# Loading modulation weights as bf16, moving border matmuls, and reading the post-norm factor from PSUM in a two-layer conv/attention step on eight cores

## The chip, the cores and the metric

The kernel runs on the eight cores of one Trainium2 chip. Each core works on its own batch element, with no exchange between cores. The metric is device time in microseconds (us) of the slowest core, as the median of several executions. Some executions fall into a slow state, in which the cores of one die or both show a lower granted TensorE clock. Those executions are set aside, and only fast runs are compared.

A word on names. TensorE is PE, its weight loads are PEld, VectorE is DVE, ScalarE is ACT, and GpSimd is POOL. SyncE is SP, which here only issues DMAs. "Pool queue" means the DMAs that POOL issues. Only these convert f32 to bf16 on the way in this kernel.

## The reference

Each core has three units of 1024 tokens: S0 and S1 (two halves of one latent sequence) and P (four context sequences of 256). There are two layers. Layer 0 mixes tokens with a gated convolution, layer 1 with attention. Each is followed by a gated ConvFFN.

```python
mod = silu(c) @ mod_w[i] + mod_b[i]            # 6 parts of 1024: shift, scale, gate, twice
u = rms_norm(h, g_pre) * (1 + scale) + shift
y = short_conv_mixer(u) or block_attention(u) @ w_o
h = h + gate * rms_norm(y, g_post)             # the "tail" below
u = rms_norm(h, g_pre2) * (1 + scale2) + shift2
g, up = split(dwconv3(u @ w_up))               # 2 x 2816 columns
h = h + gate2 * rms_norm((silu(g) * up) @ w_down, g_post2)
```

The width-3 convolution couples S0 and S1 at one column, the border. Whichever unit is computed first needs one column of its neighbour. For each weight block, "border matmuls" with a single right-hand column compute it.

## The kernel before

All operations go into a list scheduler written in Python. It estimates durations and fixes each engine's order. Engines execute in that order and wait on semaphores. Stages follow each other: conv input and conv output for S0, S1, P; FFN input and output for S1, P, S0; the attention stretch; then FFN input and output for S0, S1, P again. Five parts matter here.

Modulation weights in the prologue come as f32 over SP and are cast by ACT and DVE:

```python
def mod_stage(l, blks):
    ...
        P.dma("sp", d[blk][0], modw[l, blk], 128 * 8192, writes=d[blk][1])
# in mod_gen:
    if blk % 2: P.act(2048, "sb", sk, wk, w, src, AF.Copy)
    else:       P.dve(lambda e, ...: e.tensor_copy(out=w, in_=src), 1024, sk, wk)
```

FFN input takes its weights from a ring of 23 KB per partition, 4 KB per block. Border matmuls get a scheduling priority 18 us later than their block and hold its weight slot until they have run:

```python
for c in range(NCF):                       # 22
    w, wk = load_w(wup[l, c], KC * 256)    # pool queue, f32 -> bf16
    for s in range(2):
        zmm(b, ub, ..., wk, halo=s * 22 + c, late=18.0)   # 16 matmuls of 128x512
        P.act(1024, "ps", ..., r, z, AF.Copy, scale=...)
        taps(U, r, z, ...)                                # two DVE ops that read PSUM
```

The tail of every output phase scales y with rs, the reciprocal RMS. It reads rs from SBUF, and POOL adds the result to h:

```python
rs = rs_t[:, (2 + ct) * 512:(3 + ct) * 512]
rstd_ops(6 + ct, 512, D, rs, rk)           # ACT: Ln, then Exp
for m in range(KC):
    P.dve(... e.scalar_tensor_tensor(out=y, in0=y, scalar=cf[...], in1=rs, op0=mult, op1=mult) ...)
    P.pool(... tensor_tensor(out=hh, in0=hh, in1=y, op=add) ...)
```

The last output phase runs column half by column half and loads every weight twice. The modulation blocks of layer 0 are spread like this:

```python
stage(conv_in(S0, UU, True), ..., (mod_gen(0, [2, 3]), 1, 0.8), (load_h(S1, x_in, 1), 0, 0.5))
stage(conv_in(S1, UU, False), ..., (mod_gen(0, [4]), 2, 1.0), (load_h(PU, x_in, 0), 3, 0.5))
stage(conv_in(PU, UU, False), ..., (mod_gen(0, [5]), 0, 1.0))
```

## Time and profile before

The median was 2769.04 us. The profiled execution took 2773.4 us on core 5, the slowest. These lines of the page show the busy time of each engine, the granted TensorE clock in 40 slices (9 means 90 to 99 per cent), and four groups of instructions. A group gives line, engine, operation, output and inputs, shape and count, then total busy us, mean ns of one, and the idle time before them.

```profile
PE 2549.2 (92%) x13935; PEld 1167.3 (42%) x13935; DVE 1466.2 (53%) x1497; ACT 1303.9 (47%) x1739; POOL 1021.2 (37%) x971
...
PEclk9999999989999999999999999999999999999998
...
L606 PE MATMUL ps<-u,wr 128*128 128x512 bf16 x5376 | 1208.3, 385 | 85.3 <-DVE ra L631 23.4
...
L549 DVE SCALAR_TENSOR_TENSOR yb<-yb,coef,rs 128x512 f32<-128x512 f32 x96 | 127.7, 1360 | 248.3 <-ACT rs L100 248.3
...
L549 DVE SCALAR_TENSOR_TENSOR ev<-ev,coef,rs 128x512 f32<-128x512 f32 x80 | 110.3, 1409 | 178.6 <-ACT rs L100 178.6
...
L553 POOL TENSOR_TENSOR h<-h,yb 128x512 f32<-128x512 f32 x92 | 135.4, 1483 | 68.4 <-DVE yb L549 67.9
```

The clock line: a 9 stands for 90% or more of full speed.

The view of PE's waits for the same core gives who was waited for, total us, times and the longest wait:

```profile
PE ps L606 <- DVE ra L631: 23.4, 20, 3.7
PE ps L606 <- DMA wr<-win: 18.8, 6, 4.9
PE ps L606 <- DMA wr<-wup: 17.9, 5, 4.7
PE ps L384 <- ACT u L100: 15.1, 4, 5.3
```

L606 is the projection matmul of the conv and FFN inputs. It waits for tap results on DVE, for conv weights (win) and for FFN weights (wup). L384 is the modulation matmul, which waits for ACT's casts.

### The profile page before, as it was taken

How to read it: one execution, taken by the hardware profiler on the slowest of the kernel's cores; microseconds unless marked ns; L12 is line 12 of the kernel's file. 1: busy time of each engine (PE TensorE's matmuls, PEld its weight loads, DVE VectorE, ACT ScalarE, POOL GpSimd, SP SyncE). 2: the span in 40 equal slices, each digit the busy share in tenths (PEclk: the TensorE clock that was granted, in tenths of full speed). 3: DMA queues.
4: the chain of work that ended last, by engine and by line, in shares of the span. 5: the costliest groups of instructions: out<-in, count | busy, mean ns of one | idle time of the engine just before them, and what ended most of it. 6: DMA issues, size and time to landing. Idle time of an engine off the chain costs nothing.

```text
span 2773.4 us, 38402 instructions; the slowest of 8 cores (2744.9 to 2773.4 us)
## 1 busy us (share of the span) xinstructions
PE 2549.2 (92%) x13935; PEld 1167.3 (42%) x13935; DVE 1466.2 (53%) x1497; ACT 1303.9 (47%) x1739; POOL 1021.2 (37%) x971
## 2 busy tenths in 40 slices
PE   1899999889999999998997999999999999999997
PEld 0344444444444444443443444434444444444443
DVE  2446565856189638726524223243285618736743
ACT  2133324434255434436665777777543434434432
POOL 1124241734074335415425233240163316425423
PEclk9999999989999999999999999999999999999998
DMA  8557654344467545634235000100334355536456
GB/s 232 121 92 154 128 91 80 65 84 75 75 145 152 101 70 98 106 53 83 50 58 179 12 12 9 28 1 1 61 54 84 65 104 122 126 63 136 85 91 145
DMA packets 75368, 242.13 MB, mean 87 GB/s; under 512 B 9264, under 2 KB 12848, under 8 KB 74160
## 3 DMA queue, kind: packets, MB, share of 16 engines
q0 software_dynamic: 48368, 171.99, 36.8%
q1 hardware_dynamic: 26816, 67.69, 7.3%
q8 instruction: 115, 1.88, 0.3%
q14 instruction: 69, 0.57, 0.1%
HBM read 382.25 MB, written 29.36 MB: 148 GB/s over the span
## 4 chain that ended last, share of the span: by engine, by line
PE 74%; DVE 8%; DMA 7%; issue 7%; ACT 3%; POOL 1%; SPq 1%; DVEq 0%; ACTq 0%; POOLq 0%
PE ps L606 30%; PE ps L576 22%; PE ps L915 5%; PE ps L923 5%; DVE ra L631 3%; PE ps L795 3%; DMA wr<-win 2%; PE ps L932 2%; PE ps L957 2%; PE ps L585 1%; PE ps L826 1%; PE ps L484 1%; DMA yb<-modw 1%; DMA wr<-wup 1%; DVE yb L549 1%
## 5 line engine op out<-in xcount | busy, mean ns | idle before, releaser
L606 PE MATMUL ps<-u,wr 128*128 128x512 bf16 x5376 | 1208.3, 385 | 85.3 <-DVE ra L631 23.4
L606 PEld LDWEIGHTS ps<-u,wr 128*128 128x128 bf16 x5376 | 525.7, 99 | 734.8 <-issue 140.1
L576 PE MATMUL ps<-ra,wr 128*128 128x512 bf16 x2624 | 596.7, 381 | 9.2 <-DMA wr<-wdn 6.8
L631 DVE SCALAR_TENSOR_TENSOR ev<-ps,par,ev 128x1023 f32<-128x1023 f32 (+1 forms) x336 | 427.8, 1280 | 194.6 <-ACT ev L100 162.4
L576 PEld LDWEIGHTS ps<-ra,wr 128*128 128x128 bf16 x2624 | 257.3, 98 | 324.1 <-issue 20.2
L100 ACT ACTIVATE wr<-ps 128x1024 bf16<-128x1024 f32 (+1 forms) x352 | 333.6, 984 | 98.8 <-PE ps L915 96.1
L100 ACT ACTIVATE ev<-ps,par 128x1024 f32<-128x1024 f32 x168 | 186.8, 1112 | 278.8 <-PE ps L606 276.4
L549 DVE SCALAR_TENSOR_TENSOR yb<-yb,coef,rs 128x512 f32<-128x512 f32 x96 | 127.7, 1360 | 248.3 <-ACT rs L100 248.3
L712 POOL TENSOR_TENSOR ra<-ev 128x1023 bf16<-128x1023 f32 (+1 forms) x84 | 199.8, 2379 | 146.9 <-DVE ev L631 66.5
L631 DVE SCALAR_TENSOR_TENSOR ra<-ps,par,ra 128x1023 f32<-128x1023 f32 (+1 forms) x192 | 239.0, 1272 | 21.4 <-ACT ra L100 12.2
L549 DVE SCALAR_TENSOR_TENSOR ev<-ev,coef,rs 128x512 f32<-128x512 f32 x80 | 110.3, 1409 | 178.6 <-ACT rs L100 178.6
L491 DVE SCALAR_TENSOR_TENSOR tm<-h,coef,rs 128x512 f32<-128x512 f32 x192 | 146.5, 799 | 72.6 <-ACT rs L100 72.4
L923 PE MATMUL ps<-wr,ra 128*128 128x512 bf16 x640 | 175.6, 383 | 2.1 <-DVE ra L944 2.1
L482 POOL TENSOR_TENSOR sqa<-h 128x512 bf16<-128x512 f32 x104 | 117.4, 1140 | 136.5 <-PE ps L484 80.0
L100 ACT ACTIVATE sqb<-ps 128x512 bf16<-128x512 f32 x236 | 139.9, 597 | 58.8 <-PE ps L795 43.7
L553 POOL TENSOR_TENSOR h<-h,yb 128x512 f32<-128x512 f32 x92 | 135.4, 1483 | 68.4 <-DVE yb L549 67.9
L100 ACT ACTIVATE ra<-ps,par 128x1024 f32<-128x1024 f32 x96 | 106.4, 1110 | 102.9 <-PE ps L606 69.4
L100 ACT ACTIVATE yb<-ps 128x512 f32<-128x512 f32 x112 | 66.8, 596 | 183.8 <-PE ps L576 183.2
L113 POOL DMA_DIRECT2D wr<-wup x132 | 74.9, 569 | 201.3 <-PE ps L585 145.0
L553 POOL TENSOR_TENSOR h<-h,ev 128x512 f32<-128x512 f32 x80 | 114.3, 1443 | 37.9 <-DVE ev L549 37.4
L712 POOL TENSOR_TENSOR ra<-ra 128x1023 bf16<-128x1023 f32 (+1 forms) x48 | 115.8, 2412 | 30.3 <-ACT ra L100 18.7
L100 ACT ACTIVATE ev<-ps 128x512 f32<-128x512 f32 x80 | 47.6, 596 | 167.4 <-PE ps L576 163.7
(134 smaller groups left out, 2364.4 us busy)
## 6 DMA issues: line engine op xcount, KB each, us to landing
wr<-wup POOLq DMA_DIRECT2D x132, 512.0 KB, 6.0
wr<-wdn POOLq DMA_DIRECT2D x56, 704.0 KB, 7.6
wr<-modw POOLq DMA_DIRECT2D x40, 512.0 KB, 7.0
wr<-win POOLq DMA_DIRECT2D x24, 768.0 KB, 9.1
h_mem<-h SPq DMA_DIRECT2D x24, 512.0 KB, 5.5
h<-h_mem SPq DMA_DIRECT2D x24, 512.0 KB, 5.7
h_out<-h SPq DMA_DIRECT2D x48, 256.0 KB, 4.2
h<-x_in SPq DMA_DIRECT2D x16, 512.0 KB, 10.2
```

The lines of the kernel that those rows point to most:

```text
L100: return self._add("act", lambda e: e.activation(out=out, in_=in_, func=func, **kw), reads, writes, busy, busy + 0.12, table=self.TABLES.g ...
L482: P.pool(lambda e, s=s, src=src: e.tensor_tensor(out=s, in0=src, in1=src, op=ALU.mult), 512, hk(U, kc, ct), [("sqa", i)])
L491: P.dve(lambda e, kc=kc, t=t, rs=rs, src=hap(U, kc, ct * 512, ct * 512 + 512): e.scalar_tensor_tensor(out=t, in0=src, scalar=cf[:, ai, kc, ...
L549: P.dve(lambda e, y=y, m=m, rs=rs: e.scalar_tensor_tensor(out=y, in0=y, scalar=cf[:, gi, m, U.v:U.v + 1], in1=rs, op0=ALU.mult, op1=ALU.mu ...
L553: fa = lambda e, y=y, hh=hh: e.tensor_tensor(out=hh, in0=hh, in1=y, op=ALU.add)
L576: ins = e.matmul(bank(b), w3[:, k, :], rhs_fn(k, ct), start=(k == 0), stop=(k == nk - 1))
L606: ins = e.matmul(bank(b + ct), lhs_fn(kc), ub.ap[:, kc, ct * 512:ct * 512 + 512], start=(kc == 0), stop=(kc == KC - 1))
L631: P.dve(lambda e, ro=ro, zi=zi, w=w: e.scalar_tensor_tensor(out=ro, in0=zi, scalar=w, in1=ro, op0=ALU.mult, op1=ALU.add), 1024, rd + wr, wr)
L712: P.pool(lambda e, rg=rg, ru=ru, c=c: e.tensor_tensor(out=a3(c, c0, c1), in0=rg[:, c0:c1], in1=ru[:, c0:c1], op=ALU.mult), 1024, rgk + ruk ...
L795: ins = e.matmul(bank(b), w3[:, kc, :], ub.ap[:, kc, ct * 512:ct * 512 + 512], start=(kc == 0), stop=(kc == KC - 1))
L915: ins = e.matmul(o, K[:, j, k0:k0 + 128], rhs, start=True, stop=True)
L923: ins = e.matmul(bank(ob + a), V[:, c, j * 128:(j + 1) * 128], pt[:, a * 512:(a + 1) * 512], start=(ki == 0), stop=(ki == nk - 1))
```

## The change

It has five parts: (1) the first eight modulation blocks are cast by the pool queue as they load; (2) the other blocks are spread differently over the conv stages; (3) rs is left in PSUM and read there by DVE (it stays in SBUF in the attention output's tails and where the border column is taken), and the attention output's additions move from POOL to DVE; (4) the border matmuls come 1 us after their block (in FFN input S0 of layer 1 the first of them 24 us after it, and 7 us less with each block); (5) the last output keeps seven of its eight weight blocks in buffers that have become free, so that each is loaded once, and ends with two pieces of 256 columns. The diff, cut to its core:

```diff
@@ mod_stage / mod_gen
-                P.dma("sp", d[blk][0], modw[l, blk], 128 * 8192, writes=d[blk][1])
+                P.dma("pool", d[blk][0], modw[l, blk], 128 * 4096, writes=d[blk][1])
-                        if blk % 2:
-                            P.act(2048, "sb", sk, wk, w, src, AF.Copy)
-                        else:
-                            P.dve(lambda e, w=w, src=src: e.tensor_copy(out=w, in_=src), 1024, sk, wk)
+                        w, wk = staged[blk]
@@ tails
+            if on_dve or hcol:
+                rs, rk = rs_t[:, (2 + ct) * 512:(2 + ct) * 512 + n], [("rs", 2 + ct)]
+            else:
+                rs, rk = bank(b, n), pk(b)
+                if on_dve or (last and m % 2 == 1):
+                    P.dve(fa, n + 150, yk + hk(U, m, ct), hk(U, m, ct))
         def wo_out(U, qbuf, ybs, **kw):
+            kw["on_dve"] = True
@@ ffn_in
-                    zmm(..., halo=s * 22 + c, late=18.0)
+                    zmm(..., halo=s * 22 + c, late=max(1.0, late - 7.0 * c))
@@ prologue and stages
-        at(-98.0, lambda: run(load_h(S0, x_in, 0, cts=(1,), after=())))
+        at(-98.0, lambda: run(load_h(S0, x_in, 0, cts=(1,), after=staged[0][1])))
-        firstw["w"] = staged[1][1][:1]
-              (mod_gen(0, [2, 3]), 1, 0.8), (load_h(S1, x_in, 1), 0, 0.5))
+              (mod_gen(0, [2]), 2, 1.0), (load_h(S1, x_in, 1), 0, 0.5))
-              (mod_gen(0, [4]), 2, 1.0), (load_h(PU, x_in, 0), 3, 0.5))
+              (mod_gen(0, [3]), 2, 1.0), (load_h(PU, x_in, 0), 3, 0.5))
-              (mod_gen(0, [5]), 0, 1.0))
+              (mod_gen(0, [4, 5]), 0, 0.6))
-        stage(ffn_in(S0, 1, UU, True), ...
+        stage(ffn_in(S0, 1, UU, True, 24.0), ...
-        run(ffn_out(PU, 1, split=True))
+        final_out(PU, 1, S1.slot)
```

## The prediction

> **What bounds it now.** TensorE: the page gives PE 92% busy of 2773.4 us (core 5, clock 0.976); the chain of waits is 74% PE. No matmul of size goes away, so only idle PE time can be won. The timeline of PE, cut into stages, gives the idle time: 50 us before the first projection matmul (69.0 us), 17, 10 and 10 in the conv inputs, 18 and 17 in the two FFN inputs with border matmuls (194 and 190 us long), 1 to 9 in the other four, 49 in attention, 23 in the last FFN output and its tail.
>
> **What each part is worth.**
>
> 1. *Modulation loads.* Now 8 f32 blocks land at 30 to 55 us (DMA view) and are cast (1.9 us ACT, 1.2 us DVE). As bf16 on the pool queue, ahead of the conv weights, the last should land at 36 to 42 us. But the bytes read are the same and the DMA engines are full (SP alone moved 337 GB/s from 30 to 45 us). While the pool queue was busy (5 to 20 us), SP's got only 30 to 55 GB/s, so the second half of x, sent later, should still land near 58 to 60 us (58 to 64 now). Its norm costs 8 x 1.1 us of DVE. The second column half is ready near 70 instead of 77 us: **-7**.
> 2. *Spreading.* The first conv input waits 14 us for weights here (less on cores 0, 3, 4, 7). Four blocks leave it, but conv input P gets eight instead of four. **-2** net.
> 3. *rs in PSUM.* The scaling op takes 1.36 to 1.41 us on average, 0.73 at its fastest; with one SBUF and one PSUM tensor I expect 0.70 (the tap op, PSUM in, takes 1.28 for twice the length). The Trainium skill, "GPSIMD Engine Reference", Key points, says that GpSimd contends with DVE instructions with two SBUF inputs; this trace agrees, since the op slows to 4.1 us beside the pool additions. That is some 100 us of DVE, nearly all hidden. On the chain are only PE's waits for DVE taps at the start of stages, about 24 us: **-13**. The attention output's additions move to DVE and free the pool queue: **-2**.
> 4. *Borders undelayed.* Each border matmul holds its weight slot 18 us too long; the two border stages wait 9 us each for wup DMAs, the others for none. The border matmuls (some 15 us a stage) stay. **-13**. A new wait may come: banks 6 and 7 now hold rs until the tail has read it, and the first borders and modulation matmuls need them.
> 5. *Last output.* Resident weights take away 4.7 us of waits; the tail after the last matmul, 19 us, falls to about 11, as its pieces are 256 wide. 256-wide matmuls cost some 4 us more at most (0.106 to 0.124 us each, estimated from the 256-wide value projection). **-9**.
>
> Sum -46 us: **2723 us, range 2698 to 2748** (8 in 10). Faster by over 2%: 0.27; within 2%: 0.72; slower: 0.01.
>
> **What would show it.** First projection matmul before 52 us, but PE waiting for the second half until about 70. Scaling op near 0.70 us. No wup waits over 1 us in the border stages, these near 184 and 179 us. Tap waits at stage starts halved. Last output near 93 us instead of 103. DVE busy down by about 100 us.
>
> **What would make it wrong.** The second half of x landing much sooner (prologue gains 15 to 20) or starved behind conv weights (gains nothing); PE queued behind a border or modulation matmul that waits for bank 6 or 7; conv input P becoming weight-bound; the reordered schedule moving attention by more than a few us; a lower granted clock when PE idles less.

## The result, and the profile after

The changed kernel took 2689.16 us (median of 4 runs, 2688.98 to 2689.26); the kernel before took 2768.89 us (one of its four runs, 2802.52 us, was slow; the others took 2764.24 to 2769.04). The ratio is 0.9717, with a 95% interval of 0.9698 to 0.9736. A ratio here is the mean time of one kernel's fast runs over that of the other's of the same rounds, so it is not quite the ratio of the medians. The gain is 80 us, against 46 predicted, and 2689 us lies below the range of 2698 to 2748.

The lines of the page after, for core 0, the slowest this time. Projection is now L626, the scaling op L537:

```profile
PE 2526.6 (94%) x14119; PEld 1181.7 (44%) x14119; DVE 1384.5 (52%) x1549; ACT 1297.5 (48%) x1753; POOL 932.3 (35%) x931
...
PEclk9999899999999999999999999999999999999999
...
L626 PE MATMUL ps<-u,wr 128*128 128x512 bf16 x5376 | 1199.7, 383 | 43.6 <-DMA wr<-win 20.5
...
L537 DVE SCALAR_TENSOR_TENSOR ev<-ev,coef,ps 128x512 f32<-128x512 f32 x72 | 53.3, 741 | 158.3 <-ACT ps L100 156.6
```

On the page the line of yb mixes two shapes. The view of groups by form (`--lines --by-form`) keeps them apart:

```profile
L537 DVE SCALAR_TENSOR_TENSOR yb<-yb,coef,ps 128x512 f32<-128x512 f32 x56 | 41.5, 741 | 177.9 <-ACT ps L100 176.6
L537 DVE SCALAR_TENSOR_TENSOR yb<-yb,coef,ps 128x256 f32<-128x256 f32 x16 | 7.7, 479 | 26.4 <-ACT ps L100 24.9 <-DVE yb L537 0.5
```

Where rs is in PSUM, the scaling op of 512 columns fell from 1.36 to 1.41 us to 0.74 us; 0.70 was predicted. The reading from PSUM itself is not faster. Before (core 5), the 151 scaling ops that overlap a POOL operation on tensors took 1.57 us on average, and the 41 others 0.74. After (core 0), those with rs in PSUM took 0.74 us, the 113 that overlap one and the 15 that do not. What went away is the disturbance. The wait before the projection matmuls fell from 85.3 to 43.6 us. PE's waits, largest first, on core 0:

```profile
PE ps L476 <- POOL sqa L474: 21.1, 9, 9.4
PE ps L626 <- DMA wr<-win: 20.5, 7, 8.6
PE ps L504 <- ACT hsq L100: 19.2, 1, 19.2
```

The waits for wup are gone, and those for conv weights (win) are not. A wait of 19.2 us in the prologue is new.

For a finer account I cut every core's PE timeline, from PE's first matmul on, into stages. For each I took its length, PE's idle time in it, and the time that the clock records show at half clock, and averaged each over the eight cores:

| stages | length before, after | idle before, after | half clock before, after |
|---|---|---|---|
| prologue and conv stages | 467.4, 477.7 | 78.8, 87.6 | 23.0, 34.2 |
| two FFN inputs with border | 382.8, 332.3 | 35.4, 3.4 | 42.7, 0.0 |
| other four FFN inputs | 644.6, 632.9 | 20.1, 10.6 | 7.3, 6.4 |
| FFN outputs but two | 331.7, 328.1 | 2.9, 0 | 0, 0 |
| one FFN output and attention | 820.7, 807.5 | 51.5, 42.1 | 29.4, 18.8 |
| last output and tail | 103.5, 90.6 | 22.7, 10.4 | 16.3, 7.6 |
| sum | 2751, 2669 | 212, 154 | 119, 67 |

Two things stand outside the table. PE's first matmul comes at 6.8 us before and at 9.4 us after (mean of the cores), a loss of 2.6 us. And the clock records begin only where the clock first rises to full (72 and 77 us on core 0); until then the projection matmuls start 0.43 us apart, as at half clock, instead of 0.216, in both kernels.

Idle time fell by 58 us. Time at half clock fell by 52 us; for a busy PE half of that, 26 us, is lost time (somewhat less here, as the half-clock time of the tail is mostly idle). The lengths less the idle times, which is PE's busy time, fell by 24 us (2539 to 2515). Idle and busy time together fell by 82 us, and with the 2.6 us of later start that is the gain. The border stages gave 50 us of it, but only 32 us of their gain is idle time. The prologue and the conv stages, where the prediction saw 9 us of gain, lost 10, and 13 with the later start.

### The profile page after: what moved, and what is told of

It is laid out like the page before. It is cut to its first block, busy times and chain, and to the rows that moved or that the text cites. A ratio compares the mean times of both kernels' runs of the same rounds, so it can differ in the third digit from the quotient of the medians.

```text
span 2688.2 us, 38908 instructions; the slowest of 8 cores (2669.6 to 2688.2 us)
## 1 busy us (share of the span) xinstructions
PE 2526.6 (94%) x14119; PEld 1181.7 (44%) x14119; DVE 1384.5 (52%) x1549; ACT 1297.5 (48%) x1753; POOL 932.3 (35%) x931
## 4 chain that ended last, share of the span: by engine, by line
PE 85%; DMA 4%; DVE 4%; issue 3%; ACT 2%; SPq 1%; POOL 0%; DVEq 0%; ACTq 0%; POOLq 0%
PE ps L626 39%; PE ps L557 23%; PE ps L934 5%; PE ps L942 5%; PE ps L814 3%; DMA wr<-win 2%; PE ps L951 2%; PE ps L976 2%; PE ps L564 1%; PE ps L476 1%; PE ps L845 1%; DVE ra L651 1%; SPq L113 1%; DMA h<-x_in 1%; PE ps L874 1%
## 5 line engine op out<-in xcount | busy, mean ns | idle before, releaser
L626 PE MATMUL ps<-u,wr 128*128 128x512 bf16 x5376 | 1199.7, 383 | 43.6 <-DMA wr<-win 20.5
L626 PEld LDWEIGHTS ps<-u,wr 128*128 128x128 bf16 x5376 | 520.1, 98 | 670.3 <-issue 74.2
L557 PE MATMUL ps<-ra,wr 128*128 128x512 bf16 (+1 forms) x2338 | 528.4, 380 | 0.6 <-DMA wr<-wo 0.5
L557 PEld LDWEIGHTS ps<-ra,wr 128*128 128x128 bf16 x2338 | 229.7, 98 | 276.0 <-issue 9.8
L483 DVE SCALAR_TENSOR_TENSOR tm<-h,coef,rs 128x512 f32<-128x512 f32 x192 | 153.8, 836 | 70.4 <-ACT rs L100 70.4
L100 ACT ACTIVATE sqb<-ps 128x512 bf16<-128x512 f32 (+1 forms) x244 | 141.3, 583 | 54.4 <-PE ps L814 38.5
L100 ACT ACTIVATE yb<-ps 128x512 f32<-128x512 f32 (+1 forms) x120 | 68.1, 567 | 179.6 <-PE ps L557 179.0
L537 DVE SCALAR_TENSOR_TENSOR yb<-yb,coef,ps 128x512 f32<-128x512 f32 (+1 forms) x72 | 49.2, 683 | 204.4 <-ACT ps L100 201.5
L537 DVE SCALAR_TENSOR_TENSOR ev<-ev,coef,ps 128x512 f32<-128x512 f32 x72 | 53.3, 741 | 158.3 <-ACT ps L100 156.6
L539 POOL TENSOR_TENSOR h<-h,ev 128x512 f32<-128x512 f32 x72 | 94.7, 1330 | 47.8 <-DVE ev L537 47.1
L539 POOL TENSOR_TENSOR h<-h,yb 128x512 f32<-128x512 f32 (+1 forms) x76 | 92.9, 1241 | 42.1 <-DVE yb L537 41.4
```

The source lines that it names most:

```text
L100: return self._add("act", lambda e: e.activation(out=out, in_=in_, func=func, **kw), reads, writes, busy, busy + 0.12, table=self.TABLES.g ...
L483: P.dve(lambda e, kc=kc, t=t, rs=rs, src=hap(U, kc, ct * 512, ct * 512 + 512): e.scalar_tensor_tensor(out=t, in0=src, scalar=cf[:, ai, kc, ...
L537: fy = lambda e, y=y, m=m: e.scalar_tensor_tensor(out=y, in0=y, scalar=cf[:, gi, m, U.v:U.v + 1], in1=rs, op0=ALU.mult, op1=ALU.mult)
L539: fa = lambda e, y=y, hh=hh: e.tensor_tensor(out=hh, in0=hh, in1=y, op=ALU.add)
L557: ins = e.matmul(bank(b, n), w3[:, k, :], rhs(k), start=(k == 0), stop=(k == nk - 1))
L626: ins = e.matmul(bank(b + ct), lhs_fn(kc), ub.ap[:, kc, ct * 512:ct * 512 + 512], start=(kc == 0), stop=(kc == KC - 1))
```

## The experiments

The theory after the result: (a) a PE wait of more than about 2 us costs its own length and then some time at half clock, so the border change and the removed DVE waits pay more than their waits; (b) the modulation change costs time. The rival for (a) is the record's own arithmetic: a removed wait pays its length.

### Each part alone

Four kernels, each the kernel before with one part. First the border matmuls:

```diff
-                    zmm(..., halo=s * 22 + c, late=18.0)
+                    zmm(..., halo=s * 22 + c, late=max(1.0, late - 7.0 * c))
-        stage(ffn_in(S0, 1, UU, True), ffn_out(S0, 1), ...
+        stage(ffn_in(S0, 1, UU, True, 24.0), ffn_out(S0, 1), ...
```

> The kernel before with the undelayed border matmuls alone. Theory of the record (a wait costs its own length): 13 us faster than before. Rival (every PE wait of over 2 us also costs 3.4 to 6.8 us at half TensorE clock, so a removed wait pays again about half as much or more): 30 to 42 us faster; both border stages near 165 to 172 us instead of 192 and 190; time at reduced clock in them from about 21 us each to under 5, mean granted clock of a core up from 0.978 to about 0.985.

Measured: ratio 0.9859 (0.9829 to 0.9889), about 39 us faster in fast runs (2729.88 to 2736.39 us). Predicted were 13; theory (a) had 30 to 42. The view of busy time by stretch shows the two border stages on core 3: stretch, length, then busy us (count) of PE, PEld, DVE, ACT and POOL, the granted clock, the DMA share and GB/s. First the kernel before:

```profile
468.00:659.10 191.10, 174.02 (x1194) 83.65 (x1193) 129.15 (x109) 81.71 (x120) 92.45 (x88) 0.96 0.42 74
1971.70:2162.30 190.60, 173.87 (x1095) 81.86 (x1094) 133.72 (x111) 82.88 (x121) 91.08 (x82) 0.94 0.35 63
```

Then with the border part alone:

```profile
464.10:631.40 167.30, 165.50 (x1176) 81.02 (x1175) 126.32 (x108) 80.13 (x119) 94.11 (x89) 1.00 0.51 89
1941.10:2122.90 181.80, 169.38 (x1113) 80.98 (x1112) 138.10 (x111) 82.94 (x121) 91.12 (x83) 0.95 0.41 71
```

And the first of these stages in the changed kernel:

```profile
485.40:650.70 165.30, 165.30 (x1178) 81.14 (x1177) 120.81 (x108) 79.82 (x119) 90.38 (x89) 1.00 0.52 90
```

The first stage became 23.8 us shorter. PE's busy time fell by 8.5 us although the same matmuls run: the clock rose from 0.96 to 1.00. The rest is removed waiting. PE's waits on core 3, in the kernel before, for the first stage and then for the second:

```profile
PE ps L606 <- DMA wr<-wup: 8.6, 2, 6.0
...
PE ps L606 <- DVE coef L401: 2.7, 1, 2.7
PE ps L606 <- DVE modT L392: 2.7, 1, 2.7
```

```profile
PE ps L606 <- DMA wr<-wup: 8.6, 3, 3.1
PE ps L606 <- DVE ra L631: 8.1, 3, 3.7
```

With the border part alone, in the second stage:

```profile
PE ps L606 <- DVE ra L631: 12.4, 3, 6.2
```

In the second stage the weight waits are gone, but the tap waits at the start remain and even grew, so that this stage misses the 165 to 172 us that theory (a) had for it. They go away only together with part 3 (mean over the cores 190.5 us before, 181.0 with borders alone, 185.7 with part 3 alone, 167.0 with everything). Over all cores, the two stages lost 21 us of idle time and 28 us of half clock with the border part alone, and became 34 us shorter.

Next part 3 alone: rs in PSUM and the attention output's additions on DVE.

```diff
-                rs = rs_t[:, (2 + ct) * 512:(3 + ct) * 512]
-                rk = [("rs", 2 + ct)]
+                if on_dve or (hcol and ct == col // 512):
+                    rs, rk = rs_t[:, (2 + ct) * 512:(3 + ct) * 512], [("rs", 2 + ct)]
+                else:
+                    rs, rk = bank(6 + ct), pk(6 + ct)
-                    if split and ct == cts[1] and m % 2 == 0:
+                    if on_dve or (split and ct == cts[1] and m % 2 == 0):
         def wo_out(U, qbuf, ybs, **kw):
+            kw["on_dve"] = True
```

> The kernel before with rs read from PSUM in the tails and the attention output's additions on DVE, alone. Theory of the record: 15 us faster. Rival (waits plus clock): 18 to 30 us faster, from the starts of the stages conv input P, FFN inputs and from attention. Scaling op 0.70 us on average where rs is in PSUM, DVE busy down by 60 to 100 us.

Measured: two of four runs were slow, so there is no interval. The fast ones took 2732.03 and 2733.76 us, beside fast runs of the kernel before of 2766.80 to 2782.37. The mean core span of the profiled run is 39 us under that of before. The attention stretch fell from 820.7 to 808.5 us, FFN inputs S0 (layer 0) and S1 (layer 1) by 5.4 and 6.1 us, and FFN input S0 (layer 1) by 4.8; conv input S1 grew from 97.7 to 101.1. That is more than either theory expected (15, and 18 to 30).

To part the two halves of this, a later run moved the additions alone:

```diff
         def wo_out(U, qbuf, ybs, **kw):
+            kw["on_dve"] = True
```

> The kernel before with the attention output's additions on DVE alone, rs still read from SBUF. If the 12 us that the attention stretch gained with both parts come from the additions: attention 807 to 811 us instead of 821, FFN input S0 of layer 1 some 3 to 5 us shorter, 12 to 16 us faster in all, and conv input P and FFN inputs P and S0 unchanged. If they come from rs in PSUM elsewhere: no gain.

Measured: ratio 0.9912 (0.9893 to 0.9931), 24 us faster (19 by the mean core span of the profiled runs), where 12 to 16 were expected. All of the attention gain comes from the additions: the stretch fell to 806.2 us, while conv input P and FFN inputs P and S0 of layer 0 stayed. What the additions did is seen on core 7 just after the first attention output. First the kernel before, from 1450 to 1490 us, groups as on the page:

```profile
L549 DVE SCALAR_TENSOR_TENSOR ev<-ev,coef,rs 128x512 f32<-128x512 f32 x8 | 13.5, 1750 | 0.0
L549 DVE SCALAR_TENSOR_TENSOR yb<-yb,coef,rs 128x512 f32<-128x512 f32 x8 | 11.5, 1502 | 35.7 <-ACT rs L100 35.7
...
L553 POOL TENSOR_TENSOR h<-h,yb 128x512 f32<-128x512 f32 x8 | 13.4, 1702 | 7.2 <-DVE yb L549 7.2
L553 POOL TENSOR_TENSOR h<-h,ev 128x512 f32<-128x512 f32 x8 | 12.6, 1601 | 0.0
```

Then with the additions on DVE, 1445 to 1490 us:

```profile
L549 DVE SCALAR_TENSOR_TENSOR ev<-ev,coef,rs 128x512 f32<-128x512 f32 x8 | 7.8, 1001 | 0.0
L553 DVE TENSOR_TENSOR h<-h,ev 128x512 f32<-128x512 f32 x8 | 6.8, 874 | 0.0
L549 DVE SCALAR_TENSOR_TENSOR yb<-yb,coef,rs 128x512 f32<-128x512 f32 x8 | 5.7, 750 | 33.5 <-ACT rs L100 33.5
L553 DVE TENSOR_TENSOR h<-h,yb 128x512 f32<-128x512 f32 x8 | 5.3, 690 | 0.0
```

DVE has twice as many operations and is busy for the same 25.6 against 25.0 us, since scaling op and addition no longer hold each other up. The 26 us of POOL work (13.4, and 12.6 for the other half) disappear. PE's three longest waits there, 4.21 and 2.34 us for rotary work on DVE and 2.72 us for a weight load issued behind the additions, became 1.10, under 0.7 and 0.70 us. Over the eight cores, the stretch lost 11 us of idle time and 14 us of half clock. Whether the faster scaling op or the freed pool queue counts more was not tested apart. The Trainium skill, "SBUF — State Buffer", "Who interferes with whom", says that a DVE instruction with two SBUF inputs contends with a GpSimd instruction that reads SBUF, while one with at most one SBUF input, outside the 2-port performance modes, does not. The traces agree with both: with rs in SBUF 1.75 us beside the additions and 0.75 us without POOL (in the mean of 1.00 us of ev above are two ops of 1.75 us beside rotary work on POOL), with rs in PSUM 0.74 us beside POOL too.

Then the last output stage alone:

```diff
-        run(ffn_out(PU, 1, split=True))
+        final_out(PU, 1, S1.slot)
```

> The kernel before with the new last output stage alone. Both theories: the last stage 90 to 93 us instead of 103, so 10 to 13 us faster, nothing elsewhere.

Measured: ratio 0.9960 (0.9936 to 0.9984), 11 us faster; the stage fell from 103.5 to 90.6 us, as foreseen. But FFN input P just before it, where no change was expected, grew from 153.9 to 157.8 us: PE waits there 5.2 us for taps on core 0, instead of 1.1.

Then the modulation change alone, with the diff of parts 1 and 2 above:

> The kernel before with the modulation change (cast loads in the prologue, blocks spread over the stages) alone. Theory of the record: 9 us faster (7 in the prologue, 2 from spreading). Rival, from comparing stages of the two profiles: the prologue gains nothing, conv inputs S1 and P lose 4 and 10 us, conv input S0 gains 4, so 5 to 14 us slower.

Measured: ratio 1.0037 (1.0009 to 1.0065), 10 us slower. The first projection matmul comes at 72.7 us instead of 67.4 (mean of the cores); conv input S0 fell from 109.1 to 104.2, S1 is unchanged at 97.8 (the loss expected there came with part 3 instead), P grew from 96.9 to 102.5. Alone, the parts give -39, -39, -11 and +10 us, -79 together, and the whole change gives -80. In sum they add up, though single stages do not, as the second border stage showed.

### Does a wait cost more than its length?

A first test left the waits in the kernel before and let PE work in them: 72 useless matmuls in front of waits of the border stages. They are issued before the wait on the weights, and every engine's order stays as it was.

```diff
+                if o.pre:
+                    wait(e, {k: v for k, v in need.items() if k[:2] != "d_"})
+                    o.pre(self.engs[e])          # 9 or 18 matmuls with ones, results overwritten
                 wait(e, need)
+                fill = ({8: 18, 11: 9, 15: 9, 19: 9} if l == 0 else {11: 9, 15: 9, 19: 9}).get(c, 0) if first else 0
```

> The kernel before, instruction for instruction, with 72 useless matmuls of 128x512 (15.6 us of TensorE work at full clock) put in front of the seven weight waits of the two border stages, so that TensorE works while it waits; the waits for the weights themselves stay. If a wait costs only its own length: no gain, between 0 and 4 us slower. If the idle time also costs clock: time at half clock in the two stages falls from 21 and 22 us to about 0 to 4 and 6 to 10, and the kernel gets 10 to 17 us faster although it does more work.

Measured: ratio 0.9997 (0.9970 to 1.0023), so the expected gain is missing. The two stages on core 3, to be read against 191.10 and 190.60 us above:

```profile
465.80:657.60 191.80, 181.08 (x1239) 87.02 (x1238) 129.11 (x109) 81.67 (x120) 92.50 (x88) 0.97 0.41 74
1975.70:2160.50 184.80, 173.94 (x1123) 82.58 (x1122) 133.68 (x111) 82.87 (x121) 91.17 (x82) 0.97 0.36 65
```

PE's waits in the first of them with the fill:

```profile
PE ps L609 <- DVE modT L395: 2.7, 1, 2.7
PE ps L609 <- DVE coef L404: 2.7, 1, 2.7
PE ps L609 <- DMA wr<-wup: 2.2, 3, 0.9
```

The second stage did what theory (a) says: it became 5.8 us shorter with 5.8 us more work (27 matmuls of 0.216 us), since the clock rose from 0.94 to 0.97. The first stage did not. Two of its four fills stand before waits for DVE (modT and coef) which are 2.7 us long with and without the fill: these are round trips through DVE that begin when PE gets there, so the fill only postponed them. This was a flaw of my experiment. Yet at the first stage's two weight waits, which the fill did shorten on core 3 (6.0 and 2.6 us to 0.8 and 0.5), the half-clock records of 6.8 and 3.4 us went away, while those at the two waits of 2.7 us stayed. So the clock follows the waits in both stages, but a gain of time is seen in one alone.

So the second test put waits in where there are none: in the changed kernel, FFN input S1 of both layers, four times each, PE waits for an ACT instruction of a chosen length that itself waits for PE.

```diff
+                if o.pre:
+                    self.engs["act"].wait_ge(self.sems["pe"], cnt["pe"])
+                    o.pre(self.engs["act"]).then_inc(self.pause, 1)   # 256 or 3072 elements into a free buffer
+                    self.engs["pe"].wait_ge(self.pause, self.npause)
```

> The changed kernel with eight short waits of TensorE put in on purpose, four in FFN input S1 of each layer (which wait for almost nothing: 165.3 and 153.0 us): TensorE waits for a ScalarE instruction of 256 elements that itself waits for TensorE. Each wait about 1.0 to 1.6 us. Both theories: the two stages grow by the waits alone, 4 to 6.5 us each, time at half clock stays near 0 to 3 us.

> The same with an instruction of 3072 elements, so that each wait is about 3.3 to 4 us. If a wait costs its own length: the two stages grow by 13 to 16 us each. If a wait of over 2 us also costs half clock for 3.4 to 6.8 us after it: time at half clock rises to 14 to 27 us in each stage, and each grows by 20 to 29 us, that is by the waits plus half the time at half clock.

The first stage on core 3, to be read against 165.30 us in the changed kernel. With the short waits:

```profile
496.10:668.40 172.30, 165.78 (x1176) 81.22 (x1175) 120.80 (x108) 80.79 (x123) 90.30 (x89) 1.00 0.51 86
```

With the long ones:

```profile
485.20:675.00 189.80, 173.99 (x1177) 83.21 (x1176) 120.79 (x108) 90.11 (x123) 90.38 (x89) 0.95 0.45 79
```

Four waits of 1.5 to 1.7 us (6.5 us in all) made the stage 7.0 us longer, at full clock. Four of 3.9 to 4.05 us (15.8 us) made it 24.5 us longer, and PE's busy time rose by 8.7 us with the same work. On all eight cores the half-clock time in this stage was 0 with the short waits and 20.5 to 23.9 us with the long ones. In layer 1 the waits came out at 0.9 and 3.2 us. Those of 3.2 us set off 3.4 or 6.8 us of half clock per stage of four waits, and that stage grew by 16 us (mean). The whole kernels took 2700.48 to 2707.92 and 2734.26 to 2748.58 us in fast runs, against 2689 for the changed kernel. A wait of 4 us costs some 6 us here, one of 3.2 us some 4 us; one of 1.6 us costs about its length. The rival falls.

The undisturbed trace of before says the same: of 37 PE gaps of 2.0 to 2.5 us on its eight cores from the first projection matmul on, 70% are followed by half clock, of 127 gaps of 1.0 to 1.5 us 22%, and of 18 gaps of over 4.5 us all. (A gap counts as followed when a half-clock record overlaps it or begins within 3.4 us of its end. Of gaps with no other one of over 0.5 us in the 7 us before and the 3.5 us after, it is 21 of 27, 5 of 53 and all 15.) The Trainium skill, "TensorE: Matmul & The Clock Gate", Part 1, has this gate, with half clock after an idle window of about 3.4 us. The half-clock records here last 3.4 us or multiples of it, which agrees.

### Why the prologue did not gain

The prologue in the changed kernel, lines from the timeline of core 0 (start, us, engine, what; in brackets the idle time before it and what ended it):

```profile
7.24 0.76 SPq L113 DMA_DIRECT2D hcol<-x_in  x1
...
11.39 45.15 SPq L113 DMA_DIRECT2D h<-x_in  x8
...
57.13 0.21 ACT L100 ACTIVATE hsq<-hcol 128x8 bf16<-128x8 f32 x1 [19.59 <-DMA hcol<-x_in]
...
71.75 3.57 PE L626 MATMUL ps<-u,wr 128*128 128x512 bf16 x8 [5.73 <-DVE u L495]
```

In the kernel before (core 5) ACT did not stand still for the border column, and the first projection matmul came at 69.0 us:

```profile
64.34 0.19 ACT L100 ACTIVATE hsq<-hcol 128x8 bf16<-128x8 f32 x1
```

The last modulation block landed at 38.8 us, as predicted. But the border column hcol (4 KB in 1024 pieces) landed only at 57.0 us, and ACT stood still for it for 19.6 us with the norm behind it. From 35 to 50 us the SP queue moved 149 to 156 pieces per 5 us, of 4 bytes each, and the pool queue 149 to 160: they take turns, piece by piece, while a pool piece takes some 0.5 us. The Trainium skill, "DMA: Bandwidth & Descriptors", "Queues, rings and completion order", says that a DMA engine goes round its queues packet by packet; this trace agrees. First theory: send hcol first.

```diff
-        P.dma("sp", hcol_t, x_in[:, :, 1024], 4096, writes=[("hcol",)], ...)
+        at(-102.0, lambda: P.dma("sp", hcol_t, x_in[:, :, 1024], 4096, writes=[("hcol",)], ...))
```

> The changed kernel with the 4 KB load of the border column (1024 pieces of 4 bytes) sent first on its queue instead of between the two halves of x. Theory: that load alone holds up the queue from 37 to 57 us, since each piece waits its turn behind a weight packet, and ScalarE waits for it. First projection matmul then near 50 to 55 us instead of 72, conv input in full flow near 72 instead of 80: prologue plus conv input S0 8 us shorter or more, so 7 to 12 us faster than the changed kernel. Rival (the DMA engines are simply full until 58 us): under 3 us.

Measured: no gain. hcol landed at 4.4 us, but the first projection matmul came at 72.6 us on average instead of 71.7, and the time was 2688.09 to 2707.01 us in three fast runs (ratio to before 0.9728, 0.9679 to 0.9777; two runs were slow). My theory fell. Being first, the column also cost the first half of x its start ahead of the pool queue: its last piece landed at 46.3 us instead of 36.8 (core 0). The SP queue went on at 46 to 57 GB/s beside the pool queue (35 to 55 us), and the pieces of the second half still landed at 53 to 65 us. In PE's fixed order the modulation matmuls of blocks landed at 39 us stand behind sums of squares of that half, so the last two of these blocks were computed at 58.5 and 63.2 us. The border column was only the first thing in the way; the starved second half was the next. So the next kernel put that half on the pool queue, behind the modulation blocks and ahead of the conv weights:

```diff
-        at(-98.0, lambda: run(load_h(S0, x_in, 0, cts=(1,), after=staged[0][1])))
+        at(-98.0, lambda: run(load_h(S0, x_in, 0, cts=(1,), after=(), q="pool")))
```

> As a_hcol, and the second half of x goes on the pool queue between the modulation blocks and the conv weights, so that weights not yet needed come after it. It should land at 46 to 48 us instead of 58 to 64, and the second column half be ready near 60 instead of 80: 15 to 20 us faster than the changed kernel. If the bytes themselves set the time (first weights landing later than x): under 10.

Measured: it landed at 40 to 48 us, and the first projection matmul came at 56.1 us on average instead of 71.7. Two runs were slow; the fast ones took 2678.13 and 2678.64 us. That is 15.6 us in the prologue, of which 11 us are left in all, between what the two theories expected: order matters most. The first conv weights land at 53.5 us now; on core 0 the first projection matmul waits for DVE, and a later one 5.8 us for conv weights.

Part 2 was mended by moving one modulation part to a stage with no DMA waits:

```diff
-              (mod_gen(0, [4, 5]), 0, 0.6))
+              (mod_gen(0, [4]), 2, 1.0))
-              (mod_gen(1, [1, 0]), 4, 1.6))
+              (itertools.chain(mod_gen(0, [5]), mod_gen(1, [1, 0])), 4, 1.2))
```

> The changed kernel with modulation part 5 moved out of conv input P into FFN input S1, which has no DMA waits. Conv input P back from 107 to 93 to 97 us, FFN input S1 165 still (or up to 168): 8 to 13 us faster than the changed kernel. If conv input P lost its time to something else than the eight blocks: no gain.

Measured: conv input P 91.4 us instead of 107.1, FFN input S1 166.5 instead of 165.3, but the output after it 86.5 instead of 81.8, as its first weights now queue behind modulation blocks. Fast runs: 2683.40 and 2680.62 us, ratio to before 0.9676 (0.9643 to 0.9708); two others were slow. That is 6 to 9 us under the changed kernel, where 8 to 13 were expected.

### Both mends together

> Both mends in the changed kernel: the second half of x on the pool queue ahead of the conv weights, the border column first, and modulation part 5 in FFN input S1 (started earlier than in a_spread, so that it does not meet the last output's weights). Prologue 50 us instead of 62, conv input P 91 to 95 instead of 107, last output of S1 82: 20 to 28 us faster than the changed kernel, 2660 to 2670 us.

Measured: four fast runs of 2662.41 to 2669.04 us, ratio to before 0.9607 (0.9585 to 0.9628); four others were slow. That beats both kernels: 110 us under before and some 25 us under the changed kernel (2664.4 us is the mean, 2689.2 the other's median, from another call). The profiled run was slow, but its cores 4 to 7 were undisturbed. On these the first projection matmul came at 55.8 us, conv input P took 90.8 us and the output after FFN input S1 81.8 us, near what was expected.

## Why the prediction was wrong

- **Direction and most mechanisms were right, the sum was not.** -46 us was predicted, all of it idle time of PE; -80 was measured, made of 58 us less idle time and 24 us less busy time, less 2.6 us of later start. Faster by over 2% had been given only 0.27.
- **The step that failed most: "No matmul of size goes away, so only idle PE time can be won."** Half-clock time fell by 52 us, and PE's busy time with it by 24 us, which the prediction did not count. It had the clock only as a risk in the other direction. The inserted waits show that this cost follows from long waits.
- **Borders, "-13".** Measured -39 alone, with 21 us less idle time in the two stages and 28 us less half clock. The 18 and 17 us of idle time that the prediction itself listed could go nearly whole (35.4 to 3.4 us with everything), but it credited only 13 of the 18 us of wup waits. The 2.7 us waits for DVE in the first stage went too, as did 21 us of half clock there. The feared wait for banks 6 and 7 did not come: the first stage has no wait left.
- **"The attention output's additions move to DVE and free the pool queue: -2."** Measured -24 alone (-19 by the mean core span). The prediction named the contention between the scaling op and POOL, but not for this place: taking POOL away makes the scaling op fast as well, and rotary work right behind it on DVE held PE for 4.2 and 2.3 us.
- **rs in PSUM, "-13".** Somewhat too small: part 3 gave 39 us by two fast runs, of which the additions are 24 (19 by the mean core span), so 15 to 20 remain. For 0.70 us expected, 0.74 was measured.
- **Modulation loads, "-7", and spreading, "-2".** Measured +10 together. The bandwidth argument was right (the second half of x landed at 58 to 64 us), but the norm of the first half did not run early, and the first projection matmul, foreseen before 52 us, came at 71.7 (67.4 before). The prediction left out the border column, behind which ACT stood; with that moved, the second half of x stood in the way, and only its own move gained. Conv input P did become weight-bound, as listed among the risks.
- **Last output, "-9".** Measured -11; 90.6 us against 93 foreseen. That the two are so near is partly luck: the stage gave 13 us, and FFN input P before it lost 4.

## What to carry to other kernels

Price a TensorE wait by its length and by the clock after it: here waits under 1.7 us cost about their length and waits of 4 us half as much again, so remove or split the long ones first, and read the granted clock by stage. When two DMA queues share the engines, put what is needed first on the same queue ahead of what can wait, and keep a load of tiny pieces out of the way: 4 KB held a queue for 20 us here, though moving that load alone gained nothing. Before moving work off a busy engine to relieve it, look whether the helper slows it through SBUF: here DVE did double the operations in the same time once POOL was left out.

## What the Trainium skill lacked or had wrong

- "TensorE: Matmul & The Clock Gate", Part 1, speaks of half clock after an idle window of about 3.4 us. Here gaps of 2.0 to 2.5 us were already followed by it in 70% of 37 cases (21 of 27 with no other gap near), and waits of 3.2 us led to 3.4 or 6.8 us of half clock per four; waits of 1.5 to 1.7 us in none of 32.
- The same page tells all-core kernels with dense matmuls to budget a 13/16 clock on the default power profile (the profile of this chip is not on record). All eight cores ran dense matmuls here, and in fast runs the records show only full and half clock (mean 0.984 to 0.990 after the change). 13/16 appears only in the slow state: 679 us of it on core 0 of the last kernel's slow profile.
- "DMA: Bandwidth & Descriptors" has the turn-taking of queues by packet, but no figure of what it does to a queue of small pieces beside one of large pieces: here (10 to 55 us, core 0, border column first) 46 to 70 GB/s for pieces of 2 KB beside 127 to 147 GB/s written by the converting queue, and some 20 us for 1024 pieces of 4 bytes that took 3.3 us when sent first.
